# The row of mean squares as two float32r products with ones, in place of one float32 product

## The chip, the cores and the metric

The kernel runs on one core of a Trainium2 chip. The metric is the device time of one execution in microseconds (us); a version is judged by the median of several runs. The core has engines that each take their instructions in a fixed order: PE (the matrix engine, TensorE, with its weight loads shown apart as PEld), DVE (VectorE), ACT (ScalarE), POOL (GpSimd) and SP (SyncE, which issues most of the transfers here). They wait for each other through semaphores. "L94" is line 94 of the kernel.

## The reference

A trunk of four layers over a residual stream `x` of 256 tokens by 1024 features, all float32. Each layer adds a token mixer (0: differential attention, 1: block-sparse attention, 2: windowed grouped attention with sinks, 3: differential attention again) and then an MLP:

```
def rms_norm(x, g):
    y = xf * lax.rsqrt(jnp.mean(xf * xf, axis=-1, keepdims=True) + NORM_EPS)
    return (y * g.astype(jnp.float32)).astype(x.dtype)

def sqrelu_mlp(h, w_up, w_down):
    a = jnp.maximum(h @ w_up, 0)
    return (a * a) @ w_down

    h = h + y                       # y: the mixer of rms_norm(h, attn_norm_g[i])
    h = h + sqrelu_mlp(rms_norm(h, mlp_norm_g[i]), mlp_w_up[i], mlp_w_down[i])
```

The squared ReLU is homogeneous: if the factor of the MLP's norm is r for a token, leaving it out of `h @ w_up` and multiplying the MLP's output by r squared gives the same. So the MLP needs, per token, only 1 / (mean square + eps), and only when its output is added.

## The kernel before, in words

The stream is kept transposed: four tiles `hT[j]`, each 128 partitions by 512, hold features on the partitions and two blocks of 256 tokens side by side. Every large product is made at nearly float32 accuracy from float32r parts: a value is split into a high part (rounded to float32r) and a low part (the rest), and the products high by high, high by low and low by high are summed in PSUM. `stage` (L140 to L151) splits the weights: ACT writes `whi` (L149) and DVE writes `wlo` (L150), in halves of 128x1024, from `raw`, which SP fetches (L135). The pieces of weights are staged two ahead of their use; `whi` and `wlo` have three buffers each, so a piece's high part is written when the products with the piece three earlier have ended.

`norm_part` (L302, L303) makes the parts `hg` of the stream times the gain. `norm_sum` squares `hT[j]` on ACT (L307), adds up the four tiles on DVE (L312) and folds the two halves into `acc3`, 128x256 (L316). What is left is a sum over the 128 partitions, for each of 256 tokens.

`up_proj` makes the MLP's 4096 hidden features in 16 groups `g` of 256, each two banks `p_up` (b = 0 and 1). For each bank it runs 8 steps of two products: the high weights by the 512 columns of both parts, then the low weights by 256 columns. ACT copies half of a bank into `cross` (L692), DVE adds the other half into `relu` (L693), squares into `u` (L770); ACT and DVE split `u` into `uu` (L772, L773). `relu` is a pool of two buffers, used in turn by the squares of `norm_sum` and by the groups; a buffer is written again when its last reader has ended. After the code of each group stands `then(g)`; in layers 0 to 2 it makes the row of mean squares after group 1:

```
                if g == 1:
                    x = mean_row(n)
                    held["row"] = sb.tile([P, S], F32, tag="row", name="row", bufs=1)
                    V.reciprocal(held["row"], x)
```

`mean_row` (L335 to L341) multiplies `acc3` by a 128x128 matrix of ones on PE, which leaves the sum over the partitions in every row of `p_row`; DVE scales it and adds eps (`rowx`, L340) and takes the reciprocal (L886). The row is first used in `into`, at the end of `down_proj`'s first block (L704). Layer 3 takes another way (`mean_square`), which also uses the ones, as do twelve products at the start of the kernel that write a bank nobody reads.

The order on each engine is set before the run by a planner, which simulates the program with its own costs and starts, on each engine, what is ready and of the highest priority; `tc.high_priority()` lifts the instructions within it. A few orders between products of PE are fixed by hand (`TURNS`); none of them touches `p_up` or `p_row`. On the chip, an engine that comes to an instruction whose inputs are not ready waits, and all behind it on that engine wait too.

In the engines' order before, `p_row` stands on PE between the last product of group 1 and the first of group 2, in each of layers 0, 1 and 2.

Of the kernel before, what the change touches and what calls it, by code (L numbers as in the profile page):

```python
# [11 lines left out]
F32 = mybir.dt.float32  # L12
F32R = mybir.dt.float32r
I32 = mybir.dt.int32
AF = mybir.ActivationFunctionType
OP = mybir.AluOpType
AX = mybir.AxisListType

P = 128
D = 1024  # L20
S = 256
# [57 lines left out]
def f(ap):  # L79
    return ap.bitcast(F32)  # L80
# [28 lines left out]
def trunk(ctx: ExitStack, tc: tile.TileContext, xT, gains, lams, swa_row, fng, weights, out):  # L109
    nc = tc.nc  # L110
    V, A, G, T = nc.vector, nc.scalar, nc.gpsimd, Numbered(nc.tensor)

    cst = ctx.enter_context(tc.tile_pool(name="cst", bufs=1))
    tiny = ctx.enter_context(tc.tile_pool(name="tiny", bufs=2))
    sb = ctx.enter_context(tc.tile_pool(name="sb", bufs=2))
    ps = ctx.enter_context(tc.tile_pool(name="ps", bufs=4, space=bass.MemoryType.PSUM))

    def bank(tag, name):
        return ps.tile([P, 512], F32, tag=tag, name=name, bufs=4)
# [69 lines left out]


    ident = cst.tile([P, P], F32, name="ident")
    ones = cst.tile([P, P], F32, name="ones")
    G.memset(ones, 1.0)
    inv = np.float32(THETA) ** (-np.arange(0, 16, 2, dtype=np.float32) / np.float32(16))
    invt = cst.tile([P, NT, 8], F32, name="invt")
# [95 lines left out]
    def new_norm(gain):  # L291
        n = Normed()
        n.gain, n.both, n.acc = gain, [], None
        return n
# [40 lines left out]
    def mean_row(n):  # L335

        p = bank("wk", "p_row")
        T.matmul(p[:, :S], ones, n.acc, start=True, stop=True)
        x = sb.tile([P, S], F32, tag="rowx", name="rowx", bufs=1)
        V.tensor_scalar(x, p[:, :S], 1.0 / D, EPS, op0=OP.mult, op1=OP.add)  # L340
        return x  # L341
# [526 lines left out]
    n = new_norm(gv[:, 0, 0, :])  # L868
# [5 lines left out]
    for i in range(DEPTH):  # L874
        T.layer = i
        parts, rest = mixer_layer(i, n)
        n = new_norm(gv[:, 1, i, :])
# [3 lines left out]
        def then(g):  # L881
            if i + 1 < DEPTH:
# [4 lines that stand above are left out]
            elif g == 1:  # L887
                held["factor"] = cst.tile([P, NT], F32, name="factor")
                V.reciprocal(held["factor"], mean_square(n))

                held["res"] = [room(16 + t, [P, D], f"res{t}") for t in range(NT)]
                for j in range(4):
                    p = bank("acc", "p_res")
                    for t in range(NT):
                        for b in range(2):
                            T.transpose(p[:, S * t + P * b:S * t + P * b + P],
                                        hT[j][:, S * b + P * t:S * b + P * t + P], ident)
                    for t in range(NT):
                        A.activation(held["res"][t][:, S * j:S * j + S], p[:, S * t:S * t + S], AF.Copy)

        us = up_proj(n, then)
        if i + 1 < DEPTH:
            n = new_norm(gv[:, 0, i + 1, :])
# [82 lines left out]
```

## Time and profile before

| | |
|---|---|
| median of 3 runs | 1141.55 us (1141.24 to 1141.74) |
| the profiled execution | 1140.59 us, its span 1138.8 us |
| mean granted clock of PE | 0.998 of full speed |
| PE busy | 1130.8 us, 99% of the span |
| DVE busy | 825.9 us, 73% |
| ACT busy | 660.8 us, 58% |
| transfers | 198.66 MB, mean 174 GB/s |

The span runs from the first to the last instruction; the profiled execution's time is 1.8 us longer than it. A matrix product shows as a weight load (LDWEIGHTS, on PEld) and a MATMUL (on PE); a record of a MATMUL lasts until its results have drained, while the next one has long begun, so the distance between starts, and not the length of a record, is what a product takes of PE. A float32 product shows as two such pairs. In the timeline, each row has the start, the length, the engine, the line, the operation, the output and inputs with their shapes and types, and how many instructions were merged (x2); a bracket at the end tells how long the engine had been idle and what ended that.

### The profile page before, as it was taken

Reading aid. Unit: us, or ns where it says so; the run is one execution under the profiler, and the core shown is the slowest. Engines: PE = TensorE matmul, PEld = TensorE weight load, DVE = VectorE, ACT = ScalarE, POOL = GpSimd, SP = SyncE. Lnnn points to the kernel's source line nnn. Section 1 sums busy time; section 2 is a strip of 40 time slices with the busy share of each in tenths; the row PEclk is TensorE's granted clock in tenths of the full one; section 3 lists DMA queues with packets and bytes.
Section 4 is the critical chain, followed back from the end, with each engine's and each line's share of the span. In section 5 each row is a group of like instructions: output and inputs, shape, how many; then the busy total and the mean of one; then the engine's idle time right before and its main releaser. Section 6 shows DMA issues by size and latency. Waiting matters only on the chain.

```text
span 1138.8 us, 17024 instructions
## 1 busy us (share of the span) xinstructions
PE 1130.8 (99%) x6560; PEld 984.7 (86%) x6560; DVE 825.9 (73%) x1584; ACT 660.8 (58%) x1207; POOL 13.2 (1%) x43
## 2 busy tenths in 40 slices
PE   9999999999999999999999999999999999999997
PEld 7889888888888888888899998888888889888886
DVE  8878977656676698776569887775667788777453
ACT  7866666544476665654446765554446776665342
POOL 2000000000000000000000000000000000000000
PEclk9999999999999999999999999999999999999999
DMA  8543455555544355555563346555554434554551
GB/s 329 199 148 127 170 200 196 195 186 185 185 148 148 117 180 191 196 202 188 185 209 112 111 151 219 185 186 191 189 198 138 144 139 166 194 195 167 185 185 37
DMA packets 30608, 198.66 MB, mean 174 GB/s; under 512 B 3520, under 2 KB 5184, under 8 KB 7360
## 3 DMA queue, kind: packets, MB, share of 16 engines
q1 hardware_dynamic: 30240, 197.06, 50.3%
q8 instruction: 51, 0.84, 0.3%
q10 hardware_dynamic: 288, 0.52, 0.1%
q14 instruction: 29, 0.24, 0.1%
HBM read 196.52 MB, written 1.05 MB: 173 GB/s over the span
## 4 chain that ended last, share of the span: by engine, by line
PE 97%; DVE 1%; issue 1%; DMA 0%; ACT 0%; SPq 0%; POOL 0%; POOLq 0%; DVEq 0%
PE p_up L94 31%; PE p_down L94 23%; PE p_in L94 19%; PE p_last L94 7%; PE p_d L94 7%; PE p_s L94 3%; PE p_av L94 2%; PE p_t L97 1%; PE p_qk L97 1%; PE p_e L94 1%; DMA raw<-in_weights 0%; DVE wlo L150 0%; PE p_o L97 0%; DVE hg L303 0%; PE p_sum L94 0%
## 5 line engine op out<-in xcount | busy, mean ns | idle before, releaser
L150 DVE TENSOR_TENSOR wlo<-raw,whi 128x1024 fp32r<-128x1024 f32 (+1 forms) x374 | 446.5, 1209 | 200.7 <-ACT whi L149 199.9
L149 ACT ACTIVATE whi<-raw 128x1024 fp32r<-128x1024 f32 (+1 forms) x374 | 383.9, 1046 | 209.0 <-issue 114.6
L94 PE MATMUL p_up<-hg,whi 128*128 128x512 f32 x1024 | 356.1, 394 | 0.0
L94 PE MATMUL p_up<-hg,wlo 128*128 128x256 f32 x1024 | 283.7, 278 | 0.0
L94 PE MATMUL p_down<-uu,whi 128*128 128x512 f32 x768 | 266.4, 393 | 0.0
L94 PEld LDWEIGHTS p_up<-hg,whi 128*128 128x128 f32 x1024 | 191.7, 187 | 43.3
L94 PE MATMUL p_down<-uu,wlo 128*128 128x256 f32 x768 | 213.5, 278 | 0.0
L94 PE MATMUL p_in<-whi,hg 128*128 128x512 f32 (+1 forms) x736 | 212.5, 371 | 0.0
L94 PEld LDWEIGHTS p_up<-hg,wlo 128*128 128x128 f32 x1024 | 192.6, 188 | 0.5
L94 PEld LDWEIGHTS p_down<-uu,whi 128*128 128x128 f32 x768 | 143.9, 187 | 32.8
L94 PEld LDWEIGHTS p_in<-whi,hg 128*128 128x128 f32 x736 | 132.2, 188 | 23.0 <-DVE hg L303 0.6
L94 PEld LDWEIGHTS p_down<-uu,wlo 128*128 128x128 f32 x768 | 144.5, 188 | 0.0
L94 PE MATMUL p_in<-wlo,hg 128*128 128x512 f32 (+1 forms) x368 | 130.3, 368 | 0.2
L94 PE MATMUL p_d<-oo,whi 128*128 128x256 f32 (+1 forms) x416 | 84.6, 296 | 0.0
L772 ACT ACTIVATE uu<-u 128x512 fp32r<-128x512 f32 x64 | 40.5, 632 | 73.5 <-DVE u L770 73.5
L94 PE MATMUL p_last<-whi,uu 128*128 128x512 f32 (+1 forms) x264 | 79.4, 383 | 0.0
L94 PEld LDWEIGHTS p_in<-wlo,hg 128*128 128x128 f32 x368 | 68.8, 189 | 12.0 <-DVE wlo L150 1.0
L692 ACT ACTIVATE cross<-p_up 128x256 f32<-128x256 f32 x128 | 47.9, 374 | 37.3 <-PE p_up L94 35.3
L94 PEld LDWEIGHTS p_d<-oo,whi 128*128 128x128 f32 x416 | 66.2, 191 | 2.4 <-issue 0.3
L302 ACT ACTIVATE hg<-hT,gn 128x256 fp32r<-128x256 f32 x64 | 31.4, 503 | 61.2 <-DVE hT L705 61.2
L413 ACT ACTIVATE e<-ns,nm 128x128 f32<-128x128 f32 (+1 forms) x128 | 56.7, 446 | 12.9 <-DVE nm L410 12.9
L94 PE MATMUL p_d<-oo,wlo 128*128 128x256 f32 x224 | 63.1, 284 | 0.0
(168 smaller groups left out, 1072.8 us busy)
## 6 DMA issues: line engine op xcount, KB each, us to landing
raw<-in_weights SPq DMA_DIRECT2D x181, 1024.0 KB, 4.9
raw<-in_weights SPq DMA_DIRECT2D x8, 256.0 KB, 4.6
raw<-in_weights SPq DMA_DIRECT2D x4, 512.0 KB, 7.0
hT<-in_xT SPq DMA_DIRECT2D x8, 128.0 KB, 4.5
bias<-in_swa_row SPq DMA_DIRECT2D x1, 512.0 KB, 3.6
grow<-in_fng SPq DMA_DIRECT2D x1, 512.0 KB, 3.6
out<-res SPq DMA_DIRECT2D x4, 128.0 KB, 2.1
out<-res ACTq DMA_DIRECT2D x2, 256.0 KB, 2.2
```

The source lines that it names most:

```text
L94: return self.keep(out.tensor.name.rstrip("_0123456789"), self.engine.matmul(out, *args, **kw))
L97: return self.keep(out.tensor.name.rstrip("_0123456789"), self.engine.transpose(out, *args, **kw))
L149: A.activation(hi[:, s], raw[:, s], AF.Copy)
L150: V.tensor_tensor(lo[:, s], raw[:, s], f(hi[:, s]), op=OP.subtract)
L302: A.activation(both[:, 0], h, AF.Copy, scale=g)
L413: A.activation(e[:, s], ns[:, s], AF.Exp, bias=nm[:, t:t + 1], scale=-1.0, accum_out=l[:, t:t + 1])
L692: A.activation(cross, p[:, S:], AF.Copy)
L772: A.activation(both[:, :, 0], r3(2)(u), AF.Copy)
```

## The change

The matrix of ones is declared float32r; `ones` stays as its float32 view, for the memset and the other users. In `mean_row`, ACT copies `acc3` into a high part, DVE subtracts to get the low part, and PE makes two float32r products with the ones, accumulated in `p_row`, in place of one float32 product. The parts are a tile of the pool `relu`. The copy and the subtraction are issued at high priority.

```
-    ones = cst.tile([P, P], F32, name="ones")
+    ones_r = cst.tile([P, P], F32R, name="ones")
+    ones = f(ones_r)
...
-        T.matmul(p[:, :S], ones, n.acc, start=True, stop=True)
+        parts = sb.tile([P, 2, S], F32R, tag="relu", name="rowh")
+        with tc.high_priority():
+            A.activation(parts[:, 0], n.acc, AF.Copy)
+            V.tensor_tensor(parts[:, 1], n.acc, f(parts[:, 0]), op=OP.subtract)
+        for x in range(2):
+            T.matmul(p[:, :S], ones_r, parts[:, x], start=x == 0, stop=x == 1)
```

The planner's new order on each engine differs from the old one only around `p_row`, over some ten instructions. Names are the buffers' with the piece's or bank's number left out, and group numbers added in words.

```
layers 0 and 2
PE    last product of group 1; p_row (high part); 4 products of group 2; p_row (low part); the rest of group 2
ACT   uu (group 0); whi first half; cross (group 1, b = 1); rowh high part; whi second half; uu (group 1)
DVE   relu, relu (group 1); rowh low part; u (group 1); rowx; wlo; uu (group 1); reciprocal; wlo
layer 1
PE    last product of group 1; p_row (high part); 2 products of group 2; p_row (low part); the rest of group 2
ACT   cross (group 1, b = 0); rowh high part; uu (group 0); cross (group 1, b = 1); whi, whi
DVE   u (group 0); relu (group 1, b = 0); rowh low part; uu (group 0); relu (group 1, b = 1); rowx; u; reciprocal
```

In the old order DVE had `relu, relu, rowx, u, reciprocal, uu, wlo, wlo` in layers 0 and 2, and ACT the same without `rowh`. POOL's and SP's orders are unchanged.

## The prediction

> **What bounds the kernel now.** I read the page's busy times and chain first, then PE's waits, then the timelines of PE, ACT and DVE around each `p_row`.
>
> ```profile
> PE 1130.8 (99%) x6560; PEld 984.7 (86%) x6560; DVE 825.9 (73%) x1584; ACT 660.8 (58%) x1207; POOL 13.2 (1%) x43
> PE 97%; DVE 1%; issue 1%; DMA 0%; ACT 0%; SPq 0%; POOL 0%; POOLq 0%; DVEq 0%
> ```
>
> PE is busy for 99% of the span and 97% of the chain that ended last. So whatever PE loses in the middle is added to the time, and whatever it saves is taken off; work on DVE (73%) and ACT (58%) counts only where PE waits for it. PE's own waits are few, the longest groups by total being these (microseconds, times, longest):
>
> ```profile
> PEld p_s L94 <- DVE kpadl L556: 1.8, 8, 0.3
> PEld p_s L94 <- issue: 1.4, 5, 0.5
> PEld p_av L94 <- issue: 1.3, 6, 0.4
> ```
>
> None names `p_row` or `p_up`: before the change PE passes the row of mean squares without stopping. The chain shows what the float32 product costs PE (start, length), and PE's timeline shows it between the groups in layer 0:
>
> ```profile
> 130.81 0.43 PE p_row L94 x2
> 131.24 77.66 PE p_up L94 x448
> ```
> ```profile
> 130.53 0.28 PE L94 MATMUL p_up<-hg,wlo 128*128 128x256 f32 x1
> 130.64 0.59 PE L94 MATMUL p_row<-acc,ones 128*128 128x256 f32 x2
> ...
> 131.30 0.28 PE L94 MATMUL p_up<-hg,wlo 128*128 128x256 f32 x1
> 131.42 0.40 PE L94 MATMUL p_up<-hg,whi 128*128 128x512 f32 x1
> 131.65 0.28 PE L94 MATMUL p_up<-hg,wlo 128*128 128x256 f32 x1
> ```
>
> A float32r product of 256 columns takes 0.12 us from start to start (131.30 to 131.42), one of 512 takes 0.23 (131.42 to 131.65); the float32 product of 256 columns takes 0.43.
>
> **The change part by part.** *The products.* Per layer, one float32 product (0.43) goes and two float32r products of 256 columns come, 2 x 0.115 = 0.23, where 0.115 is from the chain's row of 448 `p_up` products: 77.66 / 224 pairs = 0.347, less 0.23 for the wide one. PE saves 0.20 us in each of layers 0 to 2, 0.6 in all. That is all the change can give, since layer 3, the warm-up products and the memset keep their float32 view and cost what they did.
>
> *The wait for the high part, layers 0 and 2.* Before, the product needed only `acc3`, which was long there. Now it needs ACT's copy, and the copy stands in ACT's queue behind the first half of `whi` and behind `cross` of group 1, b = 1. ACT in layer 0, then `acc3` on DVE:
>
> ```profile
> 128.06 0.38 ACT L692 ACTIVATE cross<-p_up 128x256 f32<-128x256 f32 x1 [0.56 <-PE p_up L94]
> 129.98 0.63 ACT L772 ACTIVATE uu<-u 128x512 fp32r<-128x512 f32 x1 [1.53 <-DVE u L770]
> 130.72 1.06 ACT L149 ACTIVATE whi<-raw 128x1024 fp32r<-128x1024 f32 x1
> 131.69 0.36 ACT L692 ACTIVATE cross<-p_up 128x256 f32<-128x256 f32 x1
> 131.95 1.05 ACT L149 ACTIVATE whi<-raw 128x1024 fp32r<-128x1024 f32 x1
> ```
> ```profile
> 127.13 0.42 DVE L316 TENSOR_TENSOR acc<-acc 128x256 f32<-128x256 f32 x1
> 129.26 0.69 DVE L770 SCALAR_TENSOR_TENSOR u<-relu 128x512 f32<-128x512 f32 x1
> 131.60 0.92 DVE L693 TENSOR_TENSOR relu<-p_up,cross 128x256 f32<-128x256 f32 x2
> ```
>
> `acc3` is ready at 127.55, and ACT even idles 1.53 us before `uu`; but in the new order the copy comes after the `cross` that starts at 131.69. This `whi` writes the buffer that group 1's weights leave, so it can't start before PE has ended group 1, at about 130.7; `cross` needs the end of group 1 too. Both are released just as PE arrives at `p_row`. So the copy takes the place where `whi`'s second half starts now, 131.95, which is 1.31 us after PE's 130.64. Its length no row shows. By size:
>
> ```profile
> L149 ACT ACTIVATE whi<-raw 128x1024 fp32r<-128x1024 f32 x366 | 378.8, 1055 | 206.4 <-issue 114.6 <-PE p_up L94 36.5 <-PE p_last L94 21.0
> L302 ACT ACTIVATE hg<-hT,gn 128x256 fp32r<-128x256 f32 x64 | 31.4, 503 | 61.2 <-DVE hT L705 61.2
> L513 ACT ACTIVATE oo<-p_av 128x256 fp32r<-128x256 f32 x16 | 5.6, 383 | 1.5 <-PE p_av L94 1.4
> L149 ACT ACTIVATE whi<-raw 128x512 fp32r<-128x512 f32 x8 | 5.0, 628 | 2.7 <-DMA raw<-in_weights 2.5
> ```
>
> The same copy takes 1055 ns for 1024 and 628 for 512 elements, so 628 - 427/2 = 415 for 256; 383 (out of PSUM) and 503 (with a scale per partition) are the ends. I take 0.415, the same operation on the same memory. It ends at 132.37. What it takes PE to restart, from the one clear case, a late low part of weights at the start (chain first, then PEld and PE):
>
> ```profile
> 22.61 0.04 issue
> 22.66 7.33 PE p_in L94 x31
> ```
> ```profile
> 22.66 0.19 PEld L94 LDWEIGHTS p_in<-wlo,hg 128*128 128x128 f32 x1 [0.50 <-DVE wlo L150]
> 22.66 0.50 PE L94 MATMUL p_in<-wlo,hg 128*128 128x512 f32 x1
> 23.00 0.63 PE L94 MATMUL p_in<-whi,hg 128*128 128x512 f32 x2
> ```
>
> 0.04 us to hand over; then the weight load starts together with its product, and the next product follows 0.34 later in place of 0.23, so the restart costs 0.11 more. The ends for it are 0 and 0.11; I take 0.11. Layer 0 loses 1.31 + 0.415 + 0.04 + 0.11 = 1.87, less the 0.20 saved: 1.67 us.
>
> A page bears on the restart. The Trainium skill, "TensorE: Matmul & The Clock Gate", in its step-by-step of a matmul, says that PE pulls weight loads ahead of products that are still running; by that the ones would be loaded during the wait, the 0.11 would go, and the sum below would be 3.36. In the row above the late operand was the moving one and the stationary `hg` had long been there, and still the load waited until 22.66, so I go by the row.
>
> In layer 2 the same instructions stand in the same order:
>
> ```profile
> 674.79 0.59 PE L94 MATMUL p_row<-acc,ones 128*128 128x256 f32 x2
> 675.83 0.37 ACT L692 ACTIVATE cross<-p_up 128x256 f32<-128x256 f32 x1
> 676.10 1.05 ACT L149 ACTIVATE whi<-raw 128x1024 fp32r<-128x1024 f32 x1
> ```
>
> 676.10 - 674.79 = 1.31 again, so again 1.67 us.
>
> *The wait for the high part, layer 1.* Here the copy stands before `uu` of group 0, in a gap of ACT. But its tile takes the buffer of group 0's `relu`, whose last reader is `u`:
>
> ```profile
> 421.42 0.59 PE L94 MATMUL p_row<-acc,ones 128*128 128x256 f32 x2
> 420.68 0.68 DVE L770 SCALAR_TENSOR_TENSOR u<-relu 128x512 f32<-128x512 f32 x1
> 421.40 0.63 ACT L772 ACTIVATE uu<-u 128x512 fp32r<-128x512 f32 x1 [1.87 <-DVE u L770]
> ```
>
> So it starts where `uu` starts now, 421.40, ends at 421.82, and PE goes on at 421.86 in place of 421.42: 0.44 + 0.11 - 0.20 = 0.35 us. In layers 0 and 2 group 0's `u` ended at 129.95, before the copy's turn, so there the buffer delays nothing.
>
> *The subtraction and the second product.* In layer 0, `relu` of b = 1 follows `cross` (end 132.05) and ends near 132.5; the subtraction then takes about as long as L316 (0.42) and ends near 132.9. PE reaches the second product four products after the first: 132.41 + 0.11 + 0.115 + 2 x 0.347 = 133.33. It costs nothing beyond its slot, 0.4 us in hand. In layer 1 only two products lie between: 421.86 + 0.11 + 0.115 + 0.347 = 422.43, against 421.86 + 0.42 = 422.28, 0.15 in hand; this is the tightest cover, and if it fails it costs tenths of a microsecond.
>
> *What stands behind the new instructions.* ACT's second `whi` half and `uu` come 0.3 to 0.4 us later, DVE's `u` about 0.5, `rowx` and the reciprocal a microsecond or two. PE uses that piece of weights two groups (11 us) later, `uu` and the row only in `down_proj`, 70 us on. Nothing there reaches PE. No transfer changes place.
>
> *The sum.* 1.67 + 0.35 + 1.67 = 3.69 us. On the profiled execution, 1140.59, that makes 1144.3; that execution lies 0.96 below the median, so on the median of 1141.55 I predict 1145.2. Low end of the terms: copy 0.383 and no restart cost, 2 x (1.31 + 0.383 + 0.04 - 0.20) + (0.423 - 0.02 - 0.20) = 3.27; high end with 503 ns, 2 x 1.76 + 0.44 = 3.97.
>
> **The rivals.** *The copy is made early, and only the saving is left.* ACT has 1.53 us idle ahead of `uu` at 129.98, with `acc3` there since 127.55. If the copy ran there, it would end by 129 and PE would never wait: 1141.55 - 0.6 = 1140.9. It decides at one point, whether the copy stands before or behind the two ACT instructions that wait for the end of group 1; the order has it behind. Chance 0.05.
>
> *The stall is given back.* If later waits of PE were for work that doesn't hang on PE, they would shrink by as much. The three longest groups come to 4.5 us in all, enough to swallow 3.69 and leave 1141.6. Against it: `kpadl` is made from PE's own transposes, and the products of weights show no wait for staging after the start; the delay moves both sides. Chance 0.09 for so much that less than 0.2% remains.
>
> *One of the long waits doesn't show*, for instance because ACT's `whi` and `cross` are released earlier there: 3.69 - 1.67 = 2.0, 1143.6. Chance 0.07.
>
> *The pause lowers PE's clock.* At the kernel's end PE's clock can be seen to fall (stretch, length, PE, granted clock):
>
> ```profile
> 1134.00:1135.00 1.00, 0.00 (x0) 1.00 0.00 0
> 1135.00:1136.00 1.00, 0.00 (x0) 0.62 0.75 262
> 1136.00:1137.00 1.00, 0.00 (x0) 0.50 0.75 262
> ```
> ```profile
> 0.98 4.86 PEld L94 LDWEIGHTS p_warm<-ones 128*128 128x128 f32 x24 [0.98 <-POOL ones L193]
> ...
> 1131.73 0.28 PE L94 MATMUL p_last<-whi,uu 128*128 128x256 f32 x1
> ```
>
> The last product ended at 1132.01, and a mean of 0.62 between 1.0 and 0.5 puts the fall at 1135.24, after 3.2 us without work. The waits here are 1.9 us. How long a fall would last, only the start bounds: 24 records of float32 warm-up products, 128 columns each, take 4.86 us, 0.20 apiece, though a record of 256 columns takes 0.43 / 2 = 0.21 later, so they run at half speed throughout. With half clock for 4.9 us, each long wait would cost 2.4 more: 1147.7 for one, 1150.1 for two. Chance 0.05. The same page, in its part on the clock gate, says that the clock is lowered after about 3.4 us of idleness in a free-running window, so 1.9 us would not do it; the trace's 3.2 agrees.
>
> **How the numbers follow.** My forecast has 0.74. Its own range is the terms' 3.27 to 3.97 on runs that spread from 1141.24 to 1141.74: 1144.5 to 1145.7. The range that holds 8 in 10 takes in the case of one long wait and one lowered clock: 1143.5 to 1147.7; left out are the two cases near no change (0.14) and the double fall of the clock. A measurement can tell some 0.2%, 2.3 us, from no change. Slower by more: my forecast, the clock, and half of the case at 1143.6, about 0.84; within: 0.15; faster by over 0.2% no case gives, 0.01.
>
> **What would show it.** Right: PE's waits name ACT's copy with about 1.8 us, twice, and 0.4 to 0.5 once; the chain passes through that copy; `p_row` products 0.12 apart from their followers; the stretch from `p_up` group 1 to group 2 longer by 1.7, 0.35 and 1.7; no wait named for the subtraction. Wrong: no wait at `p_row`, or a clock below 0.99, or waits of attention products shrunk by microseconds.

## The result

| | before | changed |
|---|---|---|
| median | 1141.49 us, 6 runs (1141.24 to 1141.74) | 1148.17 us, 6 runs (1145.36 to 1151.83) |
| profiled execution, span | 1140.59, 1138.8 us | 1151.83, 1150.0 us |

The changed kernel takes 1.006 times as long, with a 95% interval of 1.0049 to 1.007. The forecast was 1145.2, within 1143.5 to 1147.7: the sign was right, the size fell short by 3 us, and the median lies 0.5 us outside the range. The runs of before lie within 0.5 us of each other, those of the changed kernel within 6.5. Both had to be explained.

The busy times on the page of the changed kernel:

```profile
PE 1138.3 (99%) x6560; PEld 986.6 (86%) x6560; DVE 827.6 (72%) x1587; ACT 662.0 (58%) x1210; POOL 13.2 (1%) x43
```

PE is still the bound. But it is busy for 1138.3 us in place of 1130.8, 7.5 us more, with as many instructions as before. A pause is not busy time, so most of this is something beside the pause. PE's waits (microseconds, times, longest) now name the row:

```profile
PEld p_row L94 <- ACT rowh L341: 4.4, 3, 1.9
```

ACT's timeline in layer 0, then PE's:

```profile
132.87 0.36 ACT L698 ACTIVATE cross<-p_up 128x256 f32<-128x256 f32 x1
133.13 0.41 ACT L341 ACTIVATE rowh<-acc 128x256 fp32r<-128x256 f32 x1
```
```profile
131.71 0.27 PE L94 MATMUL p_up<-hg,wlo 128*128 128x256 f32 x1
133.59 0.39 PE L94 MATMUL p_row<-rowh,ones 128*128 128x256 f32 x1 [1.61 <-ACT rowh L341]
133.82 0.39 PE L94 MATMUL p_up<-hg,whi 128*128 128x512 f32 x1
134.05 0.28 PE L94 MATMUL p_up<-hg,wlo 128*128 128x256 f32 x1
...
134.52 0.28 PE L94 MATMUL p_row<-rowh,ones 128*128 128x256 f32 x1
```

The pause is the one forecast. The copy stands behind `cross`, takes 0.41 us (0.415 forecast), PE follows 0.05 after its end, and the product after it comes 0.23 later, the restart's 0.11 included. From the narrow product ahead of the row to the narrow one behind it, PE takes 131.71 to 134.05, 2.34, plus 0.12 for the second row product; before, 130.53 to 131.30, 0.77. Layer 0 loses 1.69 us by this (1.67 forecast).

What was not forecast shows in the chain, in the rows of the long stretches of layers 0, 1 and 2 behind the row (start, length):

```profile
134.80 78.44 PE p_up L94 x444
213.23 90.45 PE p_down L94 x512
...
428.78 78.79 PE p_up L94 x446
507.57 90.46 PE p_down L94 x512
...
687.37 76.96 PE p_up L94 x444
764.33 88.75 PE p_down L94 x512
```

The same 512 products, 256 pairs of a wide and a narrow one, take 88.75 us in layer 2, as in all layers before, and 90.45 in layers 0 and 1. That is 0.3467 or 0.3533 us a pair. `p_up` shows it too: 444 products in 76.96 or 78.44. PE's timeline in the middle of a group of layer 0, the wide products alone, before and changed:

```profile
150.14 0.40 PE L94 MATMUL p_up<-hg,whi 128*128 128x512 f32 x1
...
150.49 0.39 PE L94 MATMUL p_up<-hg,whi 128*128 128x512 f32 x1
...
150.83 0.40 PE L94 MATMUL p_up<-hg,whi 128*128 128x512 f32 x1
```
```profile
150.17 0.40 PE L94 MATMUL p_up<-hg,whi 128*128 128x512 f32 x1
...
150.53 0.40 PE L94 MATMUL p_up<-hg,whi 128*128 128x512 f32 x1
...
150.88 0.40 PE L94 MATMUL p_up<-hg,whi 128*128 128x512 f32 x1
```

Neither has a gap in which PE waits for anything. From wide product to wide product it goes 0.35, 0.34 in the one and 0.36, 0.35 in the other. It is not the granted clock; the two lines below are PE's row for a stretch of each (stretch, length, PE, clock, DMA share, GB/s), before first:

```profile
209.00:297.00 88.00, 88.00 (x509) 1.00 0.55 190
```
```profile
214.00:303.00 89.00, 89.00 (x505) 1.00 0.55 185
```

The clock is 1.00 and the transfers alike. I call the two the short and the long cadence; the recorded expectations below say fast and slow. A layer in the long one costs (78.44 - 76.96) + (90.45 - 88.75) = 3.2 us.

So the profiled execution's 11.2 us more of span are 3.7 of pauses (1.69 in layers 0 and 2, 0.36 in layer 1, worked out in the same way), 6.4 from two layers in the long cadence, and 1.2 from a later start, which come to 11.3. The later start is read from the chains: the first long stretch of `p_in` begins at 23.88 behind a late landing of `hT`, where before it began at 22.66. It belongs to this one execution, since in the next trace of the same kernel (below) the stretch begins at 22.88.

The other five runs have no trace here; their times fit the same bricks: 1145.36 is the pauses alone (1141.49 + 3.7), 1147.9 to 1148.4 the pauses and one layer in the long cadence. This is argued from their times, and the profiled run, the slowest of the six, is not like them.

### The profile page after: what moved, and what is told of

Same layout as the page of the kernel before. It is cut to its first block, busy times and chain, and to the rows that moved or that the text cites. A ratio compares the mean times of both kernels' runs of the same rounds, so it can differ in the third digit from the quotient of the medians.

```text
span 1150.0 us, 17031 instructions
## 1 busy us (share of the span) xinstructions
PE 1138.3 (99%) x6560; PEld 986.6 (86%) x6560; DVE 827.6 (72%) x1587; ACT 662.0 (58%) x1210; POOL 13.2 (1%) x43
## 4 chain that ended last, share of the span: by engine, by line
PE 96%; DMA 1%; DVE 1%; issue 1%; ACT 1%; SPq 0%; POOL 0%; POOLq 0%; DVEq 0%; ACTq 0%
PE p_up L94 31%; PE p_down L94 23%; PE p_in L94 18%; PE p_last L94 7%; PE p_d L94 7%; PE p_s L94 3%; PE p_av L94 2%; PE p_t L97 1%; PE p_qk L97 1%; PE p_e L94 1%; DMA hT<-in_xT 1%; DVE wlo L150 0%; PE p_o L97 0%; ACT whi L149 0%; PE p_sum L94 0%
## 5 line engine op out<-in xcount | busy, mean ns | idle before, releaser
L94 PE MATMUL p_down<-uu,whi 128*128 128x512 f32 x768 | 269.8, 397 | 0.0
```

Source lines behind the costliest of these rows:

```text
L94: return self.keep(out.tensor.name.rstrip("_0123456789"), self.engine.matmul(out, *args, **kw))
```

## The experiments

The first four kernels ran on one chip; the kernel before took 1141.10 us there (11 runs, 1140.90 to 1141.99). Theory at that point: PE's pause leaves the stream in one of two cadences. Rival: the row's new products do.

**The change again.** No edit.

> The changed kernel once more, on the chip of the next three. What is to be explained is that its runs lie between 1145.4 and 1151.8 us, with the waits for the row's high part worth 3.7 us as forecast. Theory of the cadence: after PE's pause the unchanged stream of wide and narrow products settles into one of two cadences, 0.3467 or 0.3533 us a pair, and keeps it through the layer's MLP, which costs 3.2 us where it is the slower one; so single runs lie near 1145.2, 1148.4 or 1151.6, and each layer's 512 products of the down projection take 88.75 or 90.45 us. Rival: a general disturbance of this chip or session; then the kernel before spreads as widely.

Measured: 1147.90 us (6 runs, 1147.82 to 1154.12), 1.0068 times before (1.0052 to 1.0083), while the kernel before spread over 1.1 us. So it is no matter of the session. The profiled run, 1154.12, has all three layers in the long cadence:

```profile
212.29 90.45 PE p_down L94 x512
...
506.61 90.46 PE p_down L94 x512
...
764.85 90.45 PE p_down L94 x512
```

1141.1 + 3.7 + 3 x 3.2 = 1154.4. The other five, 1147.82 to 1148.09, fit one layer: 1148.0; again the profiled run is the slowest, so no trace shows such a run. Layer 2 was short in the first trace and is long here, with the same program.

**Parts in a buffer of their own.** A pool that is idle in the MLP gives the buffer; nothing else changes in the text.

```
-        parts = sb.tile([P, 2, S], F32R, tag="relu", name="rowh")
+        parts = sb.tile([P, 2, S], F32R, tag="o", name="rowh")
```

> The parts get a buffer of another pool, idle at that time, in place of the one of relu; everything else is the change. The planner then puts the copy and the subtraction ahead of PE's need in all three layers, and both products stand side by side. If the pause causes both the waits and the slow cadence: no wait at the row's product, every layer's down projection at 88.75 us, runs as close together as those of the kernel before, and 0.6 us less than it, about 1140.9. If the two float32r products themselves upset the cadence: some layers at 90.45, and runs at 1140.9 plus 3.2 or 6.4.

Measured: 1146.56 us (5 runs, 1146.47 to 1147.62), 1.005 times before (1.0038 to 1.0062). Half right. The copy now stands ahead of `cross` of group 1, b = 0, PE waits for the row nowhere, and the products take their forecast 0.23 us. So it was the shared buffer of `relu` that made the planner put the copy late, in layers 0 and 2 too. But the time hardly falls:

```profile
131.72 0.39 PE L94 MATMUL p_row<-rowh,ones 128*128 128x256 f32 x2
131.95 0.40 PE L94 MATMUL p_up<-hg,whi 128*128 128x512 f32 x1
```
```profile
211.27 90.45 PE p_down L94 x512
...
414.51 11.27 PE p_up L94 x64
...
503.68 88.75 PE p_down L94 x512
...
758.35 90.45 PE p_down L94 x512
```

Layers 0 and 2 are in the long cadence without any pause: 1141.1 - 0.6 + 6.4 = 1146.9. Layer 1 goes the other way: the 64 products of groups 0 and 1, just ahead of its row, take 11.27 us, 0.352 a pair, and `p_down` behind it is short. The theory that the pause alone brings it has fallen.

**The pause alone.** The float32 product stays, and reads a float32 copy that ACT makes in the same place of its queue.

```
+        copied = sb.tile([P, S], F32, tag="relu", name="rowh")
+        with tc.high_priority():
+            A.activation(copied, n.acc, AF.Copy)
-        T.matmul(p[:, :S], ones, n.acc, start=True, stop=True)
+        T.matmul(p[:, :S], ones, copied, start=True, stop=True)
```

> The float32 product of before, but of a float32 copy that ACT makes at the very place in its queue where the changed kernel makes the high part. So PE pauses as there, and no float32r product comes into the stream. Pause worth 1.87 us in two layers and 0.55 in one, nothing saved: 4.3 us, 1145.8 at the least. If the pause decides the cadence: runs at 1145.8 plus 0, 3.2 or 6.4, some layers' down projection at 90.45 us. If the two products within group 2 decide it: all at 1145.8, and 88.75 in every layer.

Measured: 1145.64 us (5 runs, 1145.43 to 1146.13), 1.0039 times before (1.0026 to 1.0052). PE waits as in the changed kernel, and layers 1 and 2 are in the short cadence like layer 0, which the chain shows here:

```profile
PEld p_row L94 <- ACT rowh L340: 4.4, 3, 1.9
```
```profile
133.18 0.70 PE p_row L94 x2
...
211.54 88.75 PE p_down L94 x512
```

The pauses cost 4.5 us, 4.3 by the forecast's terms. With a float32 product behind it, the pause left the short cadence in all three layers.

**The change with an irregular place behind the row.** Group 0 runs six of its steps as wide, wide, narrow, wide, narrow, narrow; here group 2 does too.

```
-            if g == 0:
+            if g in (0, 2):
```

> The change, with the six steps that group 0 already runs out of the regular alternation (wide, wide, narrow, wide, narrow, narrow) also in group 2, behind the row's products. In both traces so far the slow cadence of the end of the output projection ends at group 0's irregular place. If an irregular place makes the stream settle in the fast cadence: all layers at 88.75 us and all runs near 1145.2. If the place has no such power: runs at 1145.2 plus multiples of 3.2, as without it.

Measured: 1155.76 us (4 runs, 1152.47 to 1156.40), 1.0122 times before (1.0108 to 1.0135): worse than all. The hope of the expectation, all layers short, fails. The profiled run is the lowest of the four; the others, 1155.63 to 1156.40, lie 3.2 to 3.9 us higher, about one more long layer. Its chain:

```profile
212.45 90.46 PE p_down L94 x512
...
505.36 88.75 PE p_down L94 x512
...
761.79 90.46 PE p_down L94 x512
...
977.55 79.08 PE p_up L94 x448
```

Layers 0 and 2 are long, layer 1 is short, and layer 3, which the change does not touch, takes 79.08 us for 448 products of `p_up`, where 77.66 is the short cadence. PE's starts around group 2 show the turn in the place itself. In layer 0, four pairs between the row and the irregular place take 1.39 us (133.90 to 135.29, 0.347 each), and behind it three take 1.06 (138.08 to 139.14, 0.353 each). Layers 2 and 3 go the same way, and layer 1 goes from long to short. So an irregular place does not set the short cadence; it can leave either, and in layer 3 it does so with no float32r row product near.

The next four kernels ran together; before took 1141.36 us there (27 runs, 1140.78 to 1142.50). Theory now: the row's float32r products move the stream from one cadence to the other.

**The parts made, the float32 product kept.** The buffer of its own, as above, and:

```
-        for x in range(2):
-            T.matmul(p[:, :S], ones_r, parts[:, x], start=x == 0, stop=x == 1)
+        T.matmul(p[:, :S], ones, n.acc, start=True, stop=True)
```

> The version with a buffer of its own for the parts, where the copy and the subtraction are made but PE keeps the float32 product of the sums; the parts are read by nobody. If the float32r products in PE's stream bring the slow cadence: the time of the kernel before, 1141.1, and 88.75 us in every layer's down projection. If the added work of ACT and DVE or the new order there brings it: the slow layers stay, 1141.1 + 6.4 = 1147.5.

Measured: 1141.45 us (11 runs, 1140.86 to 1141.92), 0.9999 times before (0.999 to 1.0008). All layers are short behind the row. ACT's and DVE's added work costs nothing that can be measured; with that work in place, it is the exchange of the products on PE that makes layers 0 and 2 long. This trace shows one thing more, in layer 1 ahead of the row (groups 0 and 1, 64 products) and behind it:

```profile
411.11 11.27 PE p_up L94 x64
422.38 0.43 PE p_row L94 x2
...
500.46 88.75 PE p_down L94 x512
```

32 pairs in 11.27 us are 0.352 each: the stream came to the row in the long cadence and left the float32 product in the short one.

**The products apart.** The buffer of its own, and the low part's product is held back until the fourth product of group 2, the order on PE that the change has in layers 0 and 2.

```
+    for layer in range(3):
+        tc.add_manual_dep(T.made[layer, "p_row"][1], T.made[layer, "p_up"][67].name, ...)
```

> The version with a buffer of its own, with the low part's product put four products of group 2 behind the high part's in all three layers: the order on PE that the changed kernel has in layers 0 and 2, without its pause. If what enters the stream, and where, decides the cadence: layers 0 and 2 alike, and the pattern differs from that of the products side by side, at 1140.5 plus 3.2 for every slow layer. If the pause made the changed kernel's slow layers: all fast, 1140.5.

Measured: 1143.99 us (11 runs, 1143.53 to 1144.48), 1.0022 times before (1.0013 to 1.0031).

```profile
209.24 88.75 PE p_down L94 x512
...
410.74 11.24 PE p_up L94 x64
...
501.35 90.45 PE p_down L94 x512
...
756.24 88.75 PE p_down L94 x512
```

The first expectation holds: layers 0 and 2 are alike, and the pattern is the opposite of the one side by side. Layers 0 and 2 stay short; layer 1 comes to the row long and stays long. 1141.36 - 0.6 + 3.2 = 1143.96. So products four apart kept the cadence, while those side by side had turned it over, from short to long or back, in each layer. With the pause, the same order in layers 0 and 2 came out long in both layers of one trace, long in one layer of another, and short in both layers of the third, the version with the irregular place, up to that place.

**One wide product.** The buffer of its own, and one product of 512 columns over both parts; ACT and DVE add the halves.

```
+        T.matmul(r3(2)(p), ones_r, parts, start=True, stop=True)
...
+        joined(x, p)
```

> The version with a buffer of its own, with one product of 512 columns over both parts in place of two of 256; ACT and DVE add the halves afterwards. PE spends the same 0.23 us per layer. If two narrow products in a row are what moves the stream into the slow cadence: all layers at 88.75 us, 1140.5. If any foreign product does: some layers at 90.45, 1140.5 plus 3.2 for each.

Measured: 1147.22 us (5 runs, 1146.64 to 1147.38), 1.005 times before (1.0037 to 1.0062).

```profile
211.15 90.46 PE p_down L94 x512
...
414.36 11.24 PE p_up L94 x64
...
503.50 88.75 PE p_down L94 x512
...
758.15 90.46 PE p_down L94 x512
```

It is long, short, long, as with two side by side, with layer 1 again long ahead of the row, and 1141.36 - 0.6 + 6.4 = 1147.2. It is not a matter of two narrow products in a row.

**An irregular place in the layers that were long.** The buffer of its own, products side by side, and:

```
-            if g == 0:
+            if g == 0 or (g == 2 and T.layer in (0, 2)):
```

> The version with a buffer of its own, with group 2 of layers 0 and 2 (the two that were slow) run with the six steps out of alternation that group 0 has. With the same steps in the pausing version the cadence changed over at that place in four layers of four. If such a place turns the cadence over: layers 0 and 2 come back to 88.75 us, layer 1 stays, and the time is 1140.5, below the kernel before. If it only ever ends in the slow one: 1146.6 as without it.

Measured: 1140.86 us (11 runs, 1140.38 to 1141.42), 0.9996 times before (0.9987 to 1.0005).

```profile
131.65 77.72 PE p_up L94 x448
209.36 88.75 PE p_down L94 x512
```

All three layers take 88.75 us for `p_down`, and layer 0 77.72 for `p_up`, 0.06 above the short cadence: the long one lasted only until the irregular place. The same edit that cost 3 us in layers 0 and 2 of the pausing version, where the stream behind the row was short, takes it back here, where it was long.

The last two ran together, before at 1141.23 us (15 runs, 1140.82 to 1142.36).

**The change with a float32 product for the low part.** The pause stays.

```
+        T.matmul(p[:, :S], ones_r, parts[:, 0], start=True, stop=False)
+        T.matmul(p[:, :S], ones, f(parts[:, 1]), start=False, stop=True)
```

> The changed kernel with its pause, only that the low part's product is a float32 product, 0.43 us in place of 0.115, in the same place of PE's order. So far the stream has been in the fast cadence behind every float32 product, whatever it was before. If the float32 product sets the fast cadence even after the pause and behind a float32r product: every layer at 88.75 us, and all runs together at 1141.3 + 3.7 + 3 x 0.315 = 1145.9. If the pause leaves the cadence to chance whatever follows: runs spread in steps of 3.2 us above 1145.9.

Measured: 1145.60 us (5 runs, 1145.48 to 1145.67), 1.0037 times before (1.0023 to 1.0051). The three layers take 88.75 us for `p_down`, here layer 1, and the runs lie within 0.2 us, where the changed kernel's lie 6 apart:

```profile
502.65 88.75 PE p_down L94 x512
```

So the float32 product leaves the short cadence behind it even after the pause and a float32r product.

**Apart where the stream is short, side by side where it is long.** As the version with the products apart, in layers 0 and 2 alone.

```
-    for layer in range(3):
+    for layer in (0, 2):
```

> The version with a buffer of its own, the low part's product four products behind the high part's in layers 0 and 2, side by side in layer 1. Reading of the runs so far, without a pause: products set apart by four keep the cadence that the stream had, products side by side turn it over; layers 0 and 2 come to the row in the fast cadence, layer 1 in the slow one. If so: all three layers at 88.75 us and the full saving of 0.6 us, 1140.7, below the kernel before. If the outcome hangs on more than that: 3.2 us more for each slow layer.

Measured: 1140.66 us (11 runs, 1140.45 to 1141.02), 0.9994 times before (0.9985 to 1.0002).

```profile
209.18 88.75 PE p_down L94 x512
...
410.73 11.27 PE p_up L94 x64
421.99 0.24 PE p_row L94 x2
...
499.89 88.75 PE p_down L94 x512
...
753.10 88.75 PE p_down L94 x512
```

The median is 0.57 us lower, just what the cheaper products were worth; the interval still touches 1, so that it beats the kernel before is likely and not shown. The edit counts on layer 1 coming to its row long, as it did in every version with a buffer of its own. In the kernel before it came short, 0.347 us a pair ahead of the row; what decides that is not known.

## Why the prediction was right and wrong

*Right, step by step.* PE as the bound; the products (0.23 in place of 0.43, full saving of 0.6 us, which the last kernel has); the copy's place, its 0.41 us and the restart's 0.11; layer 1's wait for `u` through the shared buffer; the second product without a wait. The pauses came to 1.69 + 0.36 + 1.69 = 3.74 us against 3.69, and the run of 1145.36 is, by its time, the forecast, 1145.2, with nothing added. In layer 1 the subtraction ended 0.16 us ahead of the second product, where 0.15 was forecast. Of the rivals, the early copy became real in the version with a buffer of its own, both long waits showed, the stall was not given back, and the clock stayed at 1.00 through pauses of 1.9 us. One sum in the chances is off: slower adds up to 0.825, not 0.84, and nothing hangs on it.

*On the restart,* the Trainium skill, "TensorE: Matmul & The Clock Gate", in "Step-by-step: what each phase is for", has weight loads pulled ahead of running products. At the pause the load of the ones did not come early: the wait of 4.4 us stands on the weight loads themselves, and the product behind came 0.23 us after a product that alone takes 0.12. So the 0.11 of the row stood. But this is no test of that passage: in the trace the semaphore wait stands on the weight load, both here and at 22.66 in the kernel before, and its product carries none, so it is the program that held the load back.

*Wrong:* the sentence that 0.347 us, "from the chain's row of 448 `p_up` products", is what a pair takes, and with it the one that nothing behind the new instructions reaches PE. I priced what enters the stream and took what follows it as fixed. There are 956 or so products of `p_up` and `p_down` behind the row in each layer, 478 pairs at 0.0066 us: 3.2 us a layer hang on the cadence. No term and no rival had this. The trace of the changed kernel contains it twice, and the median, by its time, once, which is the missing 3 us. The rows for it stood in the chain of the kernel before:

```profile
399.11 11.31 PE p_e L94 x64
410.42 11.16 PE p_up L94 x64
```

32 pairs of the same shapes in 11.31 us are 0.353 each, where the long stretches have 0.347; I did not compare them. So the direction came out for the forecast's reason, the pauses; the size did not, since the cadence was put at nothing.

What stays open: why the two cadences exist, and what at an irregular place or a pause picks one. The runs show only what each disturbance did: float32 products left the stream short in all the traces that have one; float32r products side by side, or one of 512 columns, turned it over; four apart, without a pause, they kept it; after a pause that order came out either way. The ten layers that turned over are only two situations repeated, layers 0 and 2 coming short and layer 1 coming long, so the kind of product is not told apart from its length (0.43 us against 0.23) or from the point of the pattern at which the stream goes on. How the stream comes to the row varies too. All twelve traces leave `p_e` in layer 1 in the long cadence, and the six pairs just ahead of that layer's row take 0.347 us each in four of them and 0.353 in eight; the two traces of the changed kernel, one program, are one of each. Which of these would hold elsewhere no run tells. That the runs without a trace differ by layers in the long cadence is argued from their times.

## What to carry to other kernels

When an engine streams without a gap, check that the same instructions take the same time per pair in every stretch of the trace, before and after a change: here a 2% change of cadence over some 165 us, 3.2 us, outweighed the 0.2 us that the new products save in a layer. A temporary that borrows another loop's buffer takes over that loop's releases, and the planner here placed it accordingly; a buffer of its own removed 4.4 us of waits in one word. And a spread of runs that grows with a change is itself a finding: steps of about 3 us between the runs pointed to the hidden term, and the chains gave its size, 3.2 us a layer.

## What the runs showed of the hardware

An unbroken alternation of float32r products of 512 and 256 columns ran in two steady cadences at a granted clock of 1.00: 88.75 or 90.45 us for 256 pairs. Each held for as long as the order was regular, some 165 us, over the seam between `p_up` and `p_down`. The trace's starts, read in nanoseconds, show two patterns: in layer 0 of the kernel before, wide products stand 350 and 343 or 344 ns apart in turn, and in layer 0 of the changed kernel 349, 350 and 361. The short cadence repeats every two pairs, the long one every three.

The Trainium skill, "TensorE: Matmul & The Clock Gate", in "Back-to-back issue gap", gives the columns at 2.4 GHz and about 2.5 ns a product, and calls this the isolated gap. By it a pair is an estimated 325 ns; here it was 347 or 353 ns, so both cadences lie above it, and which of the two is not to be had from that rule.
